# A decoder layer with 32 experts on one core: last chunk's weights split ahead, routing re-ordered, expert biases turned by TensorE

## The chip, the cores and the metric

The kernel runs on one core of one Trainium2 chip. The metric is the device time of the whole program in microseconds, lower is better. TensorE multiplies matrices, VectorE and ScalarE do elementwise work, GpSimd issues the indirect transfers, and SyncE's queue issues nearly all other transfers.

## The reference

One layer over 2048 tokens of width 1024 in fp32: three mixing branches, a gated merge, an output projection, a LayerNorm; then a router that picks 4 of 32 experts for each token, clamped-SwiGLU experts with biases, and a second LayerNorm.

```python
merged = (g_conv * (y_conv @ w_conv_proj) + g_gmlp * (y_gmlp @ w_gmlp_proj)
          + g_xa * (y_xa @ w_xa_proj))
x = layer_norm(DEEPNORM_ALPHA * x + merged @ w_out, ln1_g[l], ln1_b[l])
...
logits = (hf @ w_router + b_router).astype(jnp.float32)
top_vals, top_idx = lax.top_k(logits, TOP_K)
gate = jax.nn.softmax(top_vals, axis=-1).astype(h.dtype)
...
gu = lax.ragged_dot(xs, w_gate_up, group_sizes) + b_gate_up[sorted_expert]
g_lin, u_lin = jnp.split(gu, 2, axis=-1)
g_lin = jnp.minimum(g_lin, SWIGLU_LIMIT)
u_lin = jnp.clip(u_lin, -SWIGLU_LIMIT, SWIGLU_LIMIT)
act = (u_lin + 1) * (g_lin * jax.nn.sigmoid(SWIGLU_ALPHA * g_lin))
eo = lax.ragged_dot(act, w_down, group_sizes) + b_down[sorted_expert]
y = jnp.zeros_like(hf).at[sorted_token].add(eo * gate.reshape(-1)[order][:, None])
```

## The kernel before

Every fp32 operand is split into two parts, hi and lo: ScalarE copies the hi part (line 74), VectorE subtracts it to get the lo part (line 75), and a product is three matmuls, hi by hi, lo by hi and hi by lo. Weights come as units of 256 columns (1 MB, tile `raw`); each is split in two halves, `whi` and `wlo`. There are two `raw` buffers in the first phase and three in the experts, so a load is issued when an earlier unit has been split.

The first phase, to about 2640 us, goes over four chunks of 512 tokens. Its work is a list of items, each a weight unit with the matmuls on it (`pe`) and an epilogue (`epi`); `run_items` issues loads and splits a set number of half units ahead of the item whose matmuls it issues. A branch's last products (`proj2`, `proj3` in what follows, lines 173 to 175) are multiplied by their gates on VectorE and split (`Ah`, `Al`), because the output projection takes them as its stationary operand.

In the last chunk the output projection goes by token tiles of 128 (`last_pe`, `last_epi`): for each of four tiles 96 matmuls `lo` over two halves of the rows q and four column units j (`wo0` to `wo3`), then on VectorE the residual `r`, the LayerNorm (`ln1`) and, through TensorE, the transposes `x1T`, which are split into `Bh` and `Bl`. The router's matmuls `lg` take these. Routing of a group of tiles has three parts: `choose` makes the one-hot rows of the four chosen experts on VectorE; `place` counts each token's place with two matmuls (`pos`) and writes the lists of the experts by GpSimd; `spread` transposes the weights of the gates (`gT`). `rank` then sorts the experts by their counts, which gives `eid`, the numbers of the experts in order of size.

The experts run in a fixed order that alternates a light one (up to 128 tokens; its matmuls write `tu`, its rows are turned by `acT`) with a heavy one. Six experts are light; the heavy ones have capacities from 552 down. `schedule` puts an expert's fetch (its number, its list `lst`, its biases), the gathers of its token rows (`xg`, tiles of 128) and the preparation of each tile (`prep`: eight transposes `xsT` into two PSUM buffers, then the split into `xs`) onto the 12 steps of the expert ahead of it; with four tiles or more, the fourth preparation stands at step 10, which is step n-2. A step is one weight unit: its matmuls `up` (or `tu`), or `dn` for the down projection. All transposes, `pos`, `gT` and `lg` use one pool of two PSUM buffers, `tr_psum`.

The biases of a heavy expert's gate and up columns, `bgu`, lie with one column on each partition, since they are added per partition. `yacc` is the accumulator of the output rows in memory.

```python
self.bgu = k.sm.tile([P, 2 * KT], F32, tag="bgu", name="bgu", bufs=3)
nc.sync.dma_start(self.bgu, a["b_gate_up"][0][ds(self.reg, 1), :].rearrange("a (k p) -> p (a k)", p=P), allow_slow_non_contiguous=True)
nc.gpsimd.tensor_scalar(self.bgu[:, KT:], self.bgu[:, KT:], 1.0, None, ALU.add)
```

Of the kernel before, what the change touches and what calls it, by code (L numbers as in the profile page):

```python
# [9 lines left out]
F32 = mybir.dt.float32  # L10
F32R = mybir.dt.float32r
BF16 = mybir.dt.bfloat16
I32 = mybir.dt.int32
U32 = mybir.dt.uint32
AF = mybir.ActivationFunctionType
ALU = mybir.AluOpType
# [3 lines left out]
P = 128  # L20
D = 1024
KT = D // P
# [3 lines left out]
TT = TC // P  # L26
NE = 32
# [4 lines left out]
UC = 256  # L32
NU = D // UC
# [27 lines left out]
class Kern:  # L61
# [43 lines left out]
    def item(self, src, pe, epi=None, split=None):  # L105
        self.items.append((src, pe, epi, split or self.split_half))


    def run_items(self, first=None):
# [28 lines left out]
        for i in range(n):  # L138
            if items[i][0] is not None:
                done += 1  # L140

                split(2 * done + self.whalves - 3)
                load(ns // 2 + self.wraws)
                split(2 * done + max(2, self.whalves - 2))
            ps = items[i][1](parts.pop(i, None))

            post, self.post = self.post, []
            for f in post:
                f()
            if self.bg:  # L150
                self.bg.pop(0)()
            if items[i][2] is not None:
                items[i][2](ps)
# [47 lines left out]
    def rstd(self, pool, v, n, name, m=P):  # L201
        ve = self.nc.vector
        hv = pool.tile([P, n], F32, tag=f"hv{n}", name="hv_" + name, bufs=2)[:m]
# [330 lines left out]
    def router(self, t, th, tl):  # L534
        nc = self.nc
        te, ve = nc.tensor, nc.vector
# [5 lines left out]
        sm = self.sm  # L542
# [195 lines left out]
    def experts(self):  # L738
        exps = [Expert(self, r) for r in ORDER]

        l, h, nxt = exps[:3]
        l.number()
        h.number()

        def start(_):
            for x in (l, h):
                x.list()
            l.gather(0)
            h.gather(0)
            for x in (l, h):  # L750
                x.biases()
            l.tok_bias(0)
            l.prep(0)

# [44 lines left out]
    def overflow_table(self):  # L799
# [34 lines left out]
        ones = cp.tile([NE, P], F32, name="oones")  # L834
# [17 lines left out]
    def overflow(self):  # L852
        nc, tc = self.nc, self.tc
        n = nc.values_load(self.toti[0:1, 0:1], min_val=0, max_val=NBLK)
        with tc.For_i(0, n, 1) as i:
            e = Expert(self, None)
            e.fetch_block(i)
            e.gather(0)
            e.prep(0)
# [108 lines left out]
class Chunk:  # L968
# [12 lines left out]
    def emit(self, nxt):  # L981
# [31 lines left out]
        else:  # L1013
            self.wo = [None] * NU
            self.proj_item(2, k.vd, "pr", NU - 2)
            self.wo_item(0)
            self.wo_item(1)
            self.proj_item(2, k.vd, "pr", NU - 1)
            self.wo_item(2)
            self.wo_item(3)  # L1020
# [128 lines left out]
    def proj_item(self, b, w, src, j):  # L1149
        k = self.k  # L1150

        def pe(wt):
            return k.mm_ch(wt, *getattr(self, src), TC)
        k.item(w[:, j * UC : j * UC + UC], pe, self.proj_epi(b, j))
# [166 lines left out]
    def last_pe(self, t):  # L1321
        k, te = self.k, self.k.nc.tensor

        def pe(_):
# [3 lines left out]
            for q in range(2):  # L1328
                for j in range(NU):

                    if t >= 2 and (q, j) == (0, 1):
                        k.router(t - 2, *self.x1t[t - 2])
                    if t >= 1 and (q, j) == (1, 2):
                        self.x1_tr(t - 1)
                    hi, lo = self.wo[j][q]
# [11 lines left out]
    def last_epi(self, t):  # L1347
        k, ve = self.k, self.k.nc.vector

        def epi(ps):  # L1350
            if t == TT - 1:
                early = k.route_tasks(self.c, range(TT - 2))
                for f in early:
                    f()
            r = self.r[:, t, :]
            ve.scalar_tensor_tensor(r, r, ALPHA, ps.rearrange("p j c -> p (j c)"), ALU.mult, ALU.add)
            self.ln1(t)
            if t == TT - 1:
                third, fourth = k.route_tasks(self.c, [t - 1], ("acc", 1)), k.route_tasks(self.c, [t])
                k.router(t - 1, *self.x1t[t - 1])  # L1360
# [3 lines left out]
                k.router(t, *self.x1t[t])  # L1364
# [36 lines left out]
class Expert:  # L1401
# [22 lines left out]
    def schedule(self, n):  # L1424
# [7 lines left out]
        if self.tok:  # L1432
            todo[n - 1].append(("before", lambda: self.tok_bias(0)))
        return todo
# [17 lines left out]
    def biases(self):  # L1452
        k, nc, a = self.k, self.k.nc, self.k.a
        if self.tok:
# [3 lines left out]
            return  # L1458
        self.bgu = k.sm.tile([P, 2 * KT], F32, tag="bgu", name="bgu", bufs=3)
        nc.sync.dma_start(self.bgu, a["b_gate_up"][0][ds(self.reg, 1), :].rearrange("a (k p) -> p (a k)", p=P), allow_slow_non_contiguous=True)  # L1460
        nc.gpsimd.tensor_scalar(self.bgu[:, KT:], self.bgu[:, KT:], 1.0, None, ALU.add)
        self.xs = k.px.tile([P, KT, 2, self.C], F32R, tag="xs" + self.cls, name="xs")
# [312 lines left out]
```

## Time and profile before

| | |
|---|---|
| median of three runs | 5285.91 us (5281.21 to 5286.19) |
| profiled execution: time, span | 5280.44 us, 5278.7 us |
| mean granted TensorE clock | 0.98 of full |
| TensorE busy | 5060.7 us, 96% of the span |
| VectorE, ScalarE, GpSimd busy | 2936.3 us (56%), 2027.8 us (38%), 600.1 us (11%) |
| transfers | 794.71 MB; 766432 packets, 83416 of them under 512 bytes |

A busy share says how much of the span an engine worked; what an engine waited for, and for how long, stands in the timelines. A row of a timeline gives the start from the beginning of the span, the duration, the engine, the line of the kernel, the operation with what it writes and reads, and in brackets how long the engine was idle before it and what ended that. All times are of the one profiled execution.

### The profile page before, as it was taken

To read this page: it belongs to the slowest core of one execution; us is meant where nothing else is said; L and a number is where in the kernel's file an instruction comes from. 1 tells how busy PE (TensorE), PEld (TensorE's weight loads), DVE (VectorE), ACT (ScalarE), POOL (GpSimd) and SP (SyncE) were. 2 spreads that over 40 slices of the span, in tenths; PEclk is the share of its full clock that TensorE was granted. 3 is DMA by queue.
4 is the path that set the end of the run, shared out by engine and by line. 5 is a ranking of instruction groups with operands and counts; after the bars stand their busy time and mean duration, and the time that the engine had idled before them with its cause. 6 is when DMAs were issued, how large, how long until landed. Compare 5 with 4: busy or idle time off the path is not lost. (4 is left out here: it accounts for less than half of the span.)

```text
span 5278.7 us, 79252 instructions
## 1 busy us (share of the span) xinstructions
PE 5060.7 (96%) x32383; PEld 4633.1 (88%) x32383; DVE 2936.3 (56%) x4889; ACT 2027.8 (38%) x3011; POOL 600.1 (11%) x723
## 2 busy tenths in 40 slices
PE   9899999999999999999868999999999999999994
PEld 7788887888888888888768999999999999999984
DVE  5344346453555445543566555566666666666666
ACT  3333222332233332332234434444445555555532
POOL 0001000000010000100011112111111111211125
PEclk9899999999999999999979999999999999999997
DMA  4343332332332333322266547667666767666764
GB/s 147 123 150 132 112 112 96 112 104 93 119 109 89 112 112 104 104 88 93 87 200 205 172 127 194 187 204 205 190 181 205 207 202 207 198 205 203 210 193 128
DMA packets 766432, 794.71 MB, mean 151 GB/s; under 512 B 83416, under 2 KB 720432, under 8 KB 766064
## 3 DMA queue, kind: packets, MB, share of 16 engines
q1 hardware_dynamic: 708464, 669.78, 40.0%
q0 software_dynamic: 48000, 109.33, 8.2%
q10 hardware_dynamic: 9600, 10.49, 0.6%
q8 instruction: 257, 4.21, 0.3%
q14 instruction: 111, 0.91, 0.1%
HBM read 714.38 MB, written 75.10 MB: 150 GB/s over the span
## 5 line engine op out<-in xcount | busy, mean ns | idle before, releaser
L75 DVE TENSOR_TENSOR wlo<-raw,whi 128x1024 fp32r<-128x1024 f32 x1203 | 1450.8, 1238 | 1170.8 <-ACT whi L74 1170.5
L74 ACT ACTIVATE whi<-raw 128x1024 fp32r<-128x1024 f32 x1203 | 1220.2, 1050 | 667.0 <-PE mm L174 455.5
L173 PE MATMUL mm<-Xh,whi 128*128 128x512 f32 x1792 | 718.5, 401 | 22.1 <-ACT whi L74 22.1
L1552 PE MATMUL up<-xs,whi 128*128 128x276 f32 (+16 forms) x2304 | 724.1, 314 | 15.3 <-ACT whi L74 12.7
L1554 PE MATMUL up<-xs,wlo 128*128 128x276 f32 (+16 forms) x2304 | 721.6, 313 | 3.9 <-DVE wlo L75 3.9
L1553 PE MATMUL up<-xs,whi 128*128 128x276 f32 (+16 forms) x2304 | 720.8, 313 | 1.1 <-DVE xs L75 1.1
L175 PE MATMUL mm<-Xh,wlo 128*128 128x512 f32 x1792 | 712.9, 398 | 5.3 <-DVE wlo L75 5.2
L174 PE MATMUL mm<-Xl,whi 128*128 128x512 f32 x1792 | 708.8, 396 | 0.0
L1703 PE MATMUL dn<-whi,act 128*128 128x256 f32 (+6 forms) x2016 | 572.2, 284 | 21.1 <-ACT act L74 13.9
L1704 PE MATMUL dn<-wlo,act 128*128 128x256 f32 (+6 forms) x2016 | 569.3, 282 | 3.3 <-DVE wlo L75 3.3
L1705 PE MATMUL dn<-whi,act 128*128 128x256 f32 (+6 forms) x2016 | 568.7, 282 | 0.0
L1552 PEld LDWEIGHTS up<-xs,whi 128*128 128x128 f32 x2304 | 438.2, 190 | 24.3 <-ACT whi L74 14.4
L1734 POOL DMA_INDIRECT yacc<-yr,lst x162 | 288.9, 1783 | 1426.1 <-ACT yr L1729 1407.6
L1554 PEld LDWEIGHTS up<-xs,wlo 128*128 128x128 f32 x2304 | 438.1, 190 | 12.7 <-DVE wlo L75 6.0
L1553 PEld LDWEIGHTS up<-xs,whi 128*128 128x128 f32 x2304 | 438.5, 190 | 7.9 <-DVE xs L75 1.3
L173 PEld LDWEIGHTS mm<-Xh,whi 128*128 128x128 f32 x1792 | 338.0, 189 | 100.3 <-ACT whi L74 24.6
L175 PEld LDWEIGHTS mm<-Xh,wlo 128*128 128x128 f32 x1792 | 337.5, 188 | 91.5 <-DVE wlo L75 10.5
L174 PEld LDWEIGHTS mm<-Xl,whi 128*128 128x128 f32 x1792 | 338.2, 189 | 78.4 <-issue 0.5
L1703 PEld LDWEIGHTS dn<-whi,act 128*128 128x128 f32 (+6 forms) x2016 | 371.8, 184 | 23.4 <-ACT act L74 14.4
L1704 PEld LDWEIGHTS dn<-wlo,act 128*128 128x128 f32 (+6 forms) x2016 | 371.8, 184 | 4.8 <-DVE wlo L75 4.5
L1705 PEld LDWEIGHTS dn<-whi,act 128*128 128x128 f32 (+6 forms) x2016 | 371.7, 184 | 0.4 <-DVE act L75 0.4
L1548 PE MATMUL up<-xs,whi 128*128 128x352 f32 (+7 forms) x1280 | 370.0, 361 | 0.0
(402 smaller groups left out, 9023.4 us busy)
## 6 DMA issues: line engine op xcount, KB each, us to landing
raw<-in_w_gate_up SPq DMA_DIRECT2D x256, 1024.0 KB, 5.5
raw<-in_w_in SPq DMA_DIRECT2D x131, 1024.0 KB, 5.0
raw<-in_w_down SPq DMA_DIRECT2D x128, 1024.0 KB, 6.3
raw<-in_w_conv_proj SPq DMA_DIRECT2D x16, 1024.0 KB, 5.2
raw<-md SPq DMA_DIRECT2D x16, 1024.0 KB, 5.2
raw<-in_w_gmlp_proj SPq DMA_DIRECT2D x16, 1024.0 KB, 5.1
raw<-vd SPq DMA_DIRECT2D x16, 1024.0 KB, 5.3
raw<-in_w_out SPq DMA_DIRECT2D x16, 1024.0 KB, 6.2
```

What stands on the lines that cost most here:

```text
L74: self.nc.scalar.activation(hi, src, AF.Copy)
L75: self.nc.vector.tensor_tensor(lo, src, hi.bitcast(F32), ALU.subtract)
L173: te.matmul(o, hi[:, k, cs], xh[:, kk, :], start=first, stop=False)
L174: te.matmul(o, hi[:, k, cs], xl[:, kk, :], start=False, stop=False)
L175: te.matmul(o, lo[:, k, cs], xh[:, kk, :], start=False, stop=last)
L1548: te.matmul(o, hi[:, kk, cs], xv, start=first, stop=False)
L1552: te.matmul(o, hi[:, kk, cs], xs[:, kg, 0, s0:s1], start=first, stop=False)
L1553: te.matmul(o, hi[:, kk, cs], xs[:, kg, 1, s0:s1], start=False, stop=False)
L1554: te.matmul(o, lo[:, kk, cs], xs[:, kg, 0, s0:s1], start=False, stop=last)
L1703: te.matmul(o, ah, hi[:, kk, :], start=first, stop=False)
L1704: te.matmul(o, ah, lo[:, kk, :], start=False, stop=False)
L1705: te.matmul(o, al, hi[:, kk, :], start=False, stop=last)
```

## The change

It has five parts.

A. In the last chunk the item order becomes proj2, proj3, wo0 to wo3 instead of proj2, wo0, wo1, proj3, wo2, wo3, and proj3's item lets three more half units be split ahead of its matmuls (`ahead=3`; the method `item` stores the number).

B. The transposes of a tile's rows stand at the column unit (1, 1) of the next tile instead of (1, 2). The router's matmuls of a tile are issued ahead of the next tile's epilogue, its VectorE part in `router_tile`. For tiles 0 and 1, `choose` is issued in the epilogue of tile 2, `place` at (0, 2) of tile 3's matmuls and `spread` at (1, 3), where before all three stood ahead of tile 3's residual. The reciprocal root of one column takes 9 VectorE operations instead of 13.

C. The numbers and lists of the first two experts are issued ahead of the first expert weights.

D. `bgu` is no longer loaded by columns: the row of 2048 values is loaded as 16 rows of 128 (`brow`), TensorE turns it (`bT`, into a buffer of `tr_psum`), and VectorE copies one half and adds 1 to the other. This `bias_turn` stands after step n-2; the block of overflow experts and the first heavy expert call it on their own.

E. In the overflow table a tile of ones is taken from an existing buffer (not shown).

```diff
@@ -141,7 +142,7 @@
                 split(2 * done + self.whalves - 3)
                 load(ns // 2 + self.wraws)
-                split(2 * done + max(2, self.whalves - 2))
+                split(2 * done + max(2, self.whalves - 2) + items[i][4])
             ps = items[i][1](parts.pop(i, None))
             post, self.post = self.post, []
...
@@ -200,6 +201,19 @@
     def rstd(self, pool, v, n, name, m=P):
         ve = self.nc.vector
+
+        if n == 1:
+            h = pool.tile([P, n], F32, tag=f"hv{n}", name="hv_" + name, bufs=2)[:m]
+            ve.tensor_scalar(h, v, -0.5, -0.5 * EPS, ALU.mult, ALU.add)
+            y = pool.tile([P, n], F32, tag=f"y{n}", name="y_" + name, bufs=2)[:m]
+            s = pool.tile([P, n], F32, tag=f"s{n}", name="s_" + name, bufs=2)[:m]
+
+            ve.tensor_scalar(s.bitcast(I32), h.bitcast(I32), 1, None, ALU.logical_shift_right)
+            ve.tensor_scalar(y.bitcast(I32), s.bitcast(I32), -1.0, float(0x5F3759DF - 0x400000 + 0x40000000), ALU.mult, ALU.add)
+            for _ in range(3):
+                ve.scalar_tensor_tensor(s, y, h, y, ALU.mult, ALU.mult)
+                ve.scalar_tensor_tensor(y, s, 1.5, y, ALU.add, ALU.mult)
+            return y
         hv = pool.tile([P, n], F32, tag=f"hv{n}", name="hv_" + name, bufs=2)[:m]
         ve.tensor_scalar(hv, v, EPS, None, ALU.add)
         y = pool.tile([P, n], F32, tag=f"y{n}", name="y_" + name, bufs=2)[:m]
...
@@ -532,14 +546,16 @@
     def router(self, t, th, tl):
-        nc = self.nc
-        te, ve = nc.tensor, nc.vector
+        te = self.nc.tensor
         ps = self.tr_psum("lg")
         for k in range(KT):
             wv = self.wr[:, k, :, :].rearrange("p h e -> p (h e)")
             te.matmul(ps[:, : 2 * NE], th[:, k, :], wv, start=k == 0, stop=False)
             te.matmul(ps[:, : 2 * NE], tl[:, k, :], wv, start=False, stop=k == KT - 1)
-        sm = self.sm
+        return ps
+
+    def router_tile(self, t, ps):
+        ve, sm = self.nc.vector, self.sm
         if t == 0:
             self.v8 = sm.tile([P, TT, 8], F32, tag="v8", name="v8")
             self.i8 = sm.tile([P, TT, 8], U32, tag="i8", name="i8")
...
@@ -739,18 +755,20 @@
         exps = [Expert(self, r) for r in ORDER]
         l, h, nxt = exps[:3]
+
         l.number()
+        l.list()
         h.number()
+        h.list()
         def start(_):
-            for x in (l, h):
-                x.list()
             l.gather(0)
             h.gather(0)
             for x in (l, h):
                 x.biases()
             l.tok_bias(0)
             l.prep(0)
+            h.bias_turn()
         def prep(t):
             h.prep(t)
...
@@ -1013,11 +1033,10 @@
         else:
             self.wo = [None] * NU
             self.proj_item(2, k.vd, "pr", NU - 2)
-            self.wo_item(0)
-            self.wo_item(1)
-            self.proj_item(2, k.vd, "pr", NU - 1)
-            self.wo_item(2)
-            self.wo_item(3)
+
+            self.proj_item(2, k.vd, "pr", NU - 1, 3)
+            for j in range(NU):
+                self.wo_item(j)
             for t in range(TT):
                 k.item(None, self.last_pe(t), self.last_epi(t))
...
@@ -1328,10 +1347,12 @@
             for q in range(2):
                 for j in range(NU):
-                    if t >= 2 and (q, j) == (0, 1):
-                        k.router(t - 2, *self.x1t[t - 2])
-                    if t >= 1 and (q, j) == (1, 2):
+                    if t >= 1 and (q, j) == (1, 1):
                         self.x1_tr(t - 1)
+                    if t == TT - 1 and (q, j) == (0, 2):
+                        self.early[1]()
+                    if t == TT - 1 and (q, j) == (1, 3):
+                        self.early[2]()
                     hi, lo = self.wo[j][q]
                     for kk in range(4):
                         kg = q * 4 + kk
...
@@ -1348,20 +1369,22 @@
         k, ve = self.k, self.k.nc.vector
         def epi(ps):
-            if t == TT - 1:
-                early = k.route_tasks(self.c, range(TT - 2))
-                for f in early:
-                    f()
+            lg = k.router(t - 1, *self.x1t[t - 1]) if t else None
+            if 0 < t < TT - 1:
+                k.router_tile(t - 1, lg)
             r = self.r[:, t, :]
             ve.scalar_tensor_tensor(r, r, ALPHA, ps.rearrange("p j c -> p (j c)"), ALU.mult, ALU.add)
             self.ln1(t)
+            if t == TT - 2:
+                self.early = k.route_tasks(self.c, range(TT - 2))
+                self.early[0]()
             if t == TT - 1:
                 third, fourth = k.route_tasks(self.c, [t - 1], ("acc", 1)), k.route_tasks(self.c, [t])
-                k.router(t - 1, *self.x1t[t - 1])
+                k.router_tile(t - 1, lg)
                 third[0]()
                 self.x1_tr(t)
                 third[1]()
-                k.router(t, *self.x1t[t])
+                k.router_tile(t, k.router(t, *self.x1t[t]))
                 fourth[0]()
                 fourth[1]()
                 k.rank()
...
@@ -1431,6 +1454,7 @@
             todo[p].append(("after", lambda t=t: self.prep(t)))
         if self.tok:
             todo[n - 1].append(("before", lambda: self.tok_bias(0)))
+        todo[n - 2].append(("after", self.bias_turn))
         return todo
...
@@ -1456,10 +1480,20 @@
             if self.m < P // 2:
                 nc.vector.memset(self.xs[:, :, :, self.m :].bitcast(F32), 0.0)
             return
+        self.brow = k.sm.tile([2 * KT, P], F32, tag="brow", name="brow")
+        nc.sync.dma_start(self.brow, a["b_gate_up"][0][ds(self.reg, 1), :].rearrange("a (k p) -> (a k) p", p=P))
+        self.xs = k.px.tile([P, KT, 2, self.C], F32R, tag="xs" + self.cls, name="xs")
+
+
+    def bias_turn(self):
+        k, nc = self.k, self.k.nc
+        if self.tok:
+            return
+        pt = k.tr_psum("bT")[:, : 2 * KT]
+        nc.tensor.transpose(pt, self.brow, k.ident[: 2 * KT, : 2 * KT])
         self.bgu = k.sm.tile([P, 2 * KT], F32, tag="bgu", name="bgu", bufs=3)
-        nc.sync.dma_start(self.bgu, a["b_gate_up"][0][ds(self.reg, 1), :].rearrange("a (k p) -> p (a k)", p=P), allow_slow_non_contiguous=True)
-        nc.gpsimd.tensor_scalar(self.bgu[:, KT:], self.bgu[:, KT:], 1.0, None, ALU.add)
-        self.xs = k.px.tile([P, KT, 2, self.C], F32R, tag="xs" + self.cls, name="xs")
+        nc.vector.tensor_copy(self.bgu[:, :KT], pt[:, :KT])
+        nc.vector.tensor_scalar(self.bgu[:, KT:], pt[:, KT:], 1.0, None, ALU.add)
     def both(self, name):
...
```

The order of instructions on the engines shows where this comes to stand. First ScalarE at the end of the last chunk, from the gates of proj2's branch on, before: `Xh` and `whi` of the units wo0 and following, `Ah` the merged products' hi part.

```order
L1171 ACTIVATE gate<-mm,chan 128x512 x2
L74 ACTIVATE whi<-raw 128x1024 x2
L1171 ACTIVATE gate<-mm,chan 128x512 x2
L74 ACTIVATE Xh<-raw 128x1024 x2
L74 ACTIVATE Ah<-M 128x512 x2
L74 ACTIVATE Xh<-raw 128x1024 x2
L74 ACTIVATE whi<-raw 128x1024 x4
L74 ACTIVATE Ah<-M 128x512 x2
L74 ACTIVATE whi<-raw 128x1024
L74 ACTIVATE Bh<-raw 128x4x256
```

And now:

```order
L1190 ACTIVATE gate<-mm,chan 128x512 x2
L74 ACTIVATE whi<-raw 128x1024 x2
L1190 ACTIVATE gate<-mm,chan 128x512 x2
L74 ACTIVATE whi<-raw 128x1024 x2
L74 ACTIVATE Ah<-M 128x512 x2
L74 ACTIVATE Xh<-raw 128x1024 x4
L74 ACTIVATE whi<-raw 128x1024
L74 ACTIVATE Ah<-M 128x512 x2
L74 ACTIVATE whi<-raw 128x1024 x2
L74 ACTIVATE Bh<-raw 128x4x256
```

A pair of `whi`, proj3's weights, moved ahead of the first `Ah`, the two pairs of `Xh` (wo0 and wo1) behind it are together, and a `whi` of the next unit stands ahead of the second `Ah`, proj3's.

Second, TensorE at the routing of tiles 0 and 1, which stood behind the last matmul of tile 3 before:

```order
L1341 MATMUL lo<-Bh,Ah 128x256
L1342 MATMUL lo<-Bl,Ah 128x256
L1343 MATMUL lo<-Bh,Al 128x256
L627 LDWEIGHTS lower
L627 MATMUL pos<-rscr,lower 128x64
L628 LDWEIGHTS ones_b
L628 MATMUL pos<-rscr,ones_b 128x64
L673 MATMUL gT<-ident,rscr_19579 96x128 x2
L540 MATMUL lg<-wr,Bh 128x64
L541 MATMUL lg<-wr,Bl 128x64
L540 MATMUL lg<-wr,Bh 128x64
```

It now stands among tile 3's matmuls, 24 behind their begin:

```order
L1362 MATMUL lo<-Xh,Ah 128x256
L1363 MATMUL lo<-Xl,Ah 128x256
L1364 MATMUL lo<-Xh,Al 128x256
L643 LDWEIGHTS lower
L643 MATMUL pos<-rscr,lower 128x64
L644 LDWEIGHTS ones_b
L644 MATMUL pos<-rscr,ones_b 128x64
L1362 MATMUL lo<-whi,Ah 128x256
L1363 MATMUL lo<-wlo,Ah 128x256
L1364 MATMUL lo<-whi,Al 128x256
```

`pos` moved ahead of 72 of the tile's matmuls; `gT` follows later, at (1, 3).

Third, TensorE at the end of the preparation of the expert with 460 tokens, before: the light expert's `tu`, the last tile's transposes, then the down matmuls.

```order
L1578 MATMUL tu<-whi,xs 96x256
L1579 MATMUL tu<-wlo,xs 96x256
L1580 MATMUL tu<-whi,xs 96x256
L1527 MATMUL xsT<-ident,xg 128x76 x8
L1703 MATMUL dn<-whi,act 128x256
L1704 MATMUL dn<-wlo,act 128x256
L1705 MATMUL dn<-whi,act 128x256
```

And now:

```order
L1612 MATMUL tu<-whi,xs 96x256
L1613 MATMUL tu<-wlo,xs 96x256
L1614 MATMUL tu<-whi,xs 96x256
L1561 MATMUL xsT<-ident,xg 128x76 x8
L1493 MATMUL bT<-ident,brow 128x16
L1737 MATMUL dn<-whi,act 128x256
L1738 MATMUL dn<-wlo,act 128x256
```

`bT` came between the transposes and the down matmuls; the same stands at the other four experts with four tiles or more. On VectorE the two reads of it follow the split of that tile:

```order
L75 TENSOR_TENSOR wlo<-raw,whi 128x1024 x2
L1624 TENSOR_TENSOR Xt<-tu,bb 96x256
L1631 TENSOR_SCALAR Xt<-Xt 96x256
L75 TENSOR_TENSOR wlo<-raw,whi 128x1024 x2
L75 TENSOR_TENSOR xs<-xsT,xs 128x4x76 x2
L1495 COPY bgu<-bT 128x8
L1496 TENSOR_SCALAR bgu<-bT 128x8
L1624 TENSOR_TENSOR ut<-tu,bb 96x256
```

Only the rows of `bgu` are new there; what stands ahead of `xs` is as before.

## Rows read from the trace of the kernel before

**Rows 1.** Busy time by windows, inside the experts; the first line names the columns.

```profile
core 0: us, PE busy (x) PEld busy (x) DVE busy (x) ACT busy (x) POOL busy (x), PEclk, DMA share, GB/s
...
3600.00:3700.00 100.00, 100.00 (x740) 99.72 (x739) 65.20 (x106) 51.82 (x88) 14.11 (x14) 1.00 0.66 197
```

**Rows 2.** Timeline of TensorE, last chunk: start, duration, instruction, idle time before and releaser.

```profile
2559.60 0.80 PE L173 MATMUL mm<-Bh,whi 128*128 128x512 f32 x1 [7.73 <-ACT whi L74]
...
2574.13 0.28 PE L1341 MATMUL lo<-Xh,Ah 128*128 128x256 f32 x1
2574.25 0.28 PE L1342 MATMUL lo<-Xl,Ah 128*128 128x256 f32 x1
...
2580.13 0.38 PE L1341 MATMUL lo<-whi,Ah 128*128 128x256 f32 x1 [1.55 <-ACT whi L74]
...
2581.39 0.38 PE L1342 MATMUL lo<-wlo,Ah 128*128 128x256 f32 x1 [0.88 <-DVE wlo L75]
...
2634.59 0.63 PE L673 MATMUL gT<-ident,rscr 128*96 128x128 f32 x2 [4.52 <-DVE rscr L667]
```

**Rows 3.** Busy time by windows behind two waits of TensorE; PEclk is the granted clock.

```profile
2559.00:2566.00 7.00, 5.99 (x14) 4.26 (x15) 3.31 (x3) 1.97 (x3) 0.00 (x0) 0.51 0.72 238
...
2634.00:2636.00 2.00, 1.41 (x8) 1.43 (x8) 1.88 (x4) 0.43 (x2) 1.65 (x4) 0.52 0.01 1
```

**Rows 4.** Timeline of VectorE, last chunk and routing.

```profile
2588.82 1.22 DVE L1356 SCALAR_TENSOR_TENSOR r<-r,lo 128x1024 f32<-128x1024 f32 x1 [6.35 <-DMA r<-in_x]
...
2615.03 1.22 DVE L1356 SCALAR_TENSOR_TENSOR r<-r,lo 128x1024 f32<-128x1024 f32 x1 [1.35 <-PE lo L1343]
...
2627.66 0.15 DVE L602 TENSOR_TENSOR gt<-v 128x8 f32<-128x8 f32 x1
...
2630.11 0.49 DVE L632 TENSOR_TENSOR rscr<-pos,rscr 128x128 f32<-128x128 f32 x2
...
2634.33 1.21 DVE L1356 SCALAR_TENSOR_TENSOR r<-r,lo 128x1024 f32<-128x1024 f32 x1
...
2642.71 0.14 DVE L602 TENSOR_TENSOR gt<-v 128x4 f32<-128x4 f32 x1
```

**Rows 5.** Timelines of SyncE's queue, GpSimd and TensorE, start of the experts.

```profile
2661.24 0.90 SPq L1450 DMA_DIRECT2D lst<-lists  x2
...
2669.49 0.96 POOL L1516 DMA_INDIRECT xg<-x1d,lst  x1 [9.52 <-DMA yacc<-r]
...
2676.23 1.07 PE L1527 MATMUL xsT<-ident,xg 52*128 52x52 f32 x8 [10.66 <-DMA bb<-in_b_gate_up]
```

**Rows 6.** DMA issues by line: count, KB of each, median us to landing.

```profile
lst<-lists SPq DMA_DIRECT2D x32, 16.0 KB, 1.6
...
bgu<-in_b_gate_up SPq DMA_DIRECT2D x26, 8.0 KB, 2.9
```

**Rows 7.** Waits of TensorE in the experts: us in total, times, longest.

```profile
PE xsT L1527 <- DMA xg<-x1d,lst: 4.2, 2, 2.9
```

**Rows 8.** Timelines of TensorE and VectorE, last prep of four of the five large experts.

```profile
2845.40 0.36 PE L1703 MATMUL dn<-whi,act 128*128 128x256 f32 x1
...
2852.10 1.28 DVE L75 TENSOR_TENSOR xs<-xsT,xs 128x512 fp32r<-128x512 f32 x2
...
3036.85 0.36 PE L1703 MATMUL dn<-whi,act 128*128 128x256 f32 x1
...
3041.18 1.28 DVE L75 TENSOR_TENSOR xs<-xsT,xs 128x512 fp32r<-128x512 f32 x2
...
3400.92 0.39 PE L1703 MATMUL dn<-whi,act 128*128 128x256 f32 x1
...
3404.55 0.48 DVE L75 TENSOR_TENSOR xs<-xsT,xs 128x128 fp32r<-128x128 f32 x2
...
5030.69 0.36 PE L1703 MATMUL dn<-whi,act 128*128 128x256 f32 x1
...
5032.02 0.98 DVE L75 TENSOR_TENSOR xs<-xsT,xs 128x368 fp32r<-128x368 f32 x2
```

**Rows 9.** Timeline of TensorE behind the first of these.

```profile
2857.59 0.65 PE L1527 MATMUL xsT<-ident,xg 40*128 40x40 f32 x4 [1.84 <-DVE act L75]
```

More of the change, by code (lines that the diff above doesn't have):

```diff
@@ L103, in split_half, with item @@
         return hi, lo
-    def item(self, src, pe, epi=None, split=None):
-        self.items.append((src, pe, epi, split or self.split_half))
+    def item(self, src, pe, epi=None, split=None, ahead=0):
+        self.items.append((src, pe, epi, split or self.split_half, ahead))
     def run_items(self, first=None):
@@ L833, in overflow_table @@
         ve.tensor_scalar(mk[:, 2, :], mk[:, 0, :], self.iota_c, None, ALU.mult)
-        ones = cp.tile([NE, P], F32, name="oones")
+        ones = room[:, : NE + NBLK]
         ve.memset(ones, 1.0)
@@ L858, in overflow @@
             e.gather(0)
+            e.bias_turn()
             e.prep(0)
@@ L1147, in gate_item, with proj_item @@
         self.k.item(self.wcol(COL_G + b * D, j), self.zx, self.gate_epi(b, j))
-    def proj_item(self, b, w, src, j):
+    def proj_item(self, b, w, src, j, ahead=0):
         k = self.k
@@ L1153, in pe @@
             return k.mm_ch(wt, *getattr(self, src), TC)
-        k.item(w[:, j * UC : j * UC + UC], pe, self.proj_epi(b, j))
+        k.item(w[:, j * UC : j * UC + UC], pe, self.proj_epi(b, j), ahead=ahead)
     def projections(self, b, w, src, js):
```

## The prediction

> **What bounds the kernel now.** The page comes first: TensorE is busy for 96% of the span. The busy time by windows then says where it isn't: inside the experts it is busy for 100.00 of 100 us [rows 1], so there a microsecond that it is made to wait is a microsecond of the span, unless a later wait takes it up. Slack lies at the turn from the last chunk to the experts (about 2550 to 2800 us) and in the last norms. So I read the timelines of that turn, and then the places in the experts where the change puts an instruction into TensorE's row. The sum is made against the profiled execution, 5280.4 us (span 5278.7 and 1.7 around it); the median of the runs, 5285.9, lies 5.5 above it. A difference of 0.2%, 10.6 us, is about what a measurement of this kernel can tell from none.
>
> **A, the output weights split ahead.** Before, TensorE stands 7.73 us for proj3's first weights, and 1.55 and 0.88 us for the last output weights [rows 2]. After the first of these the granted clock is 0.51 over 7 us [rows 3], the 1.2 GHz level: 7 x 0.49 = 3.4 us lost, some 0.5 of it while idle, so about 2.9. That makes 10.2 us of waits and 2.9 of clock to be removed. I do not give all of it back. The first wait goes: proj3's whi is now ahead of the two gate epilogues in ScalarE's row. But the raw buffer for wo2 is released only by wo0's split, ScalarE now has a whi of a wo unit ahead of proj3's `Ah`, and so proj3's epilogue on VectorE starts late and wo3's split comes behind it. Laying the old durations into the new order, I find new waits of 0.9 + 1.2 us for wo2 and 5.2 + 1.3 us for wo3. The first tile's `r`, at 2588.82 before [rows 4], comes at 2583.3 to 2585.5. **A: -3.3 to -5.5; I take -4.3.**
>
> **B, the routing chain.** What it removes: before, VectorE does choose and place of tiles 0 and 1 (from 2627.66) ahead of tile 3's `r` (2634.33) [rows 4], and TensorE waits 4.52 us for their `gT` [rows 2]. Tile 2's `r` stands at 2615.03, so 19.3 us lie between the two. What it adds: `pos` now stands in TensorE's own row behind the first 24 output matmuls of tile 3, and it needs choose, which is queued on VectorE behind tile 2's whole LayerNorm. One such matmul is 0.12 us (2574.13 to 2574.25 [rows 2]). From tile 2's end TensorE has 16 router matmuls, smaller, so at most 1.9, and 24 x 0.12 = 2.9: 4.8 us. VectorE waits for the router (1.9), then does its router tile and LayerNorm (2634.33 to 2642.71 is 8.4 for the same two; four small operations fewer in the reciprocal root, which I put at 0.5) and choose (2627.66 to 2630.11, 2.45): 12.2 us. So TensorE stands about 7.4 us, and 72 matmuls, the next transposes and `gT` are queued behind the `pos` that waits. Tile 3's `r` comes 12.2 + 72 x 0.12 + about 1.6 for ten transposes (four small ones take 0.65 [rows 9]) = 22.4 us after tile 2's end, 3.1 later than before; 2.9 more where the clock falls; and the transposes of tiles 0 and 1, one step forward, meet a LayerNorm that still runs, up to 2 us. **B: +3.1 to +8.0; I take +6.3**, since 4.52 us of waiting at this very place did bring the clock to 0.52 [rows 3].
>
> **C, lists first.** The two list loads were issued at 2661.24, behind a 1 MB weight unit; the gather starts at 2669.49, and xsT stands 10.66 us until the gathered rows are there [rows 5]. A list load takes 1.6 us in the median [rows 6], so issued first the lists are there near 2663. The gather then waits for what is next late, the last rows of the accumulator, near 2666: -3.3 us. The weight unit behind the lists starts 0.7 later, which xsT's wait covers; were it not covered, C would be -2.6. **C: -3.3, or 0 where something else holds the gather.**
>
> **D, the biases as rows, is what costs.** The 26 `bgu` loads land 2.9 us after issue [rows 6]; GpSimd waits for each, with gathers queued behind it. But TensorE's waits for gathered rows are 4.2 us in all of the experts [rows 7], and that is the ceiling of what a freer GpSimd and emptier queues can give: -3, with 0 and -4.2 as ends.
>
> In their place come 26 transposes, and what matters is where they stand. In five experts, those of four tiles or more (capacities 552, 532, 460, 416 and 476), `bT` stands in TensorE's row right behind the last prep (eight xsT, two PSUM buffers) and ahead of the down matmuls. It takes one of the same two buffers, so the prep's first one must be free, and it is free when VectorE has made the first half of `xs`. VectorE reaches that late, behind two pairs of `wlo`. Before, TensorE did not care: it went straight on to `dn`, which needs nothing of this prep. Both ends are in the trace [rows 8]: when `dn` started, and when `xs` did, half of whose row frees the buffer.
> - 552: 2852.10 + 0.64 - 2845.40 = 7.3
> - 532: 3041.18 + 0.64 - 3036.85 = 5.0, and the 460 reads like it, 5.0
> - 416: 3404.55 + 0.24 - 3400.92 = 3.9
> - 476: 5032.02 + 0.49 - 5030.69 = 1.8
>
> Together 23.0 us. ScalarE and VectorE go on meanwhile, so the next waits shrink (1.84 us at 2857.59 behind the first stall [rows 9]): **+21, with 18 and 23 as ends.** The other 21 find a free buffer. Their nearest row is four transposes of 40 columns in 0.65 us [rows 9], 0.16 each, or 3.5 for the 21 with the bubble that a change of weights leaves (2.5 to 5). The two small reads on VectorE lie beside full TensorE work.
>
> **The clock behind the stalls.** After the wait of 4.52 us, which followed full work, the granted clock was 0.52, after the one of 7.73 us 0.51 over 7 us [rows 2, 3]. Four of the five stalls are of 3.9 us or more; at 2.9 each that is **+11** (0 to 11.6).
>
> Sum: -4.3 + 6.3 - 3.3 - 3.0 + 21 + 3.5 + 11 = +31.2, and 5280.4 + 31.2 = 5311.6: **5312 us**.
>
> **A rule that speaks for the change.** A `bgu` of 8 KB, 4-byte pieces, lands in 2.9 us, a list of 16 KB in 1.6 [rows 6]. The Trainium skill, page "DMA: Bandwidth & Descriptors", section "Specifications", says that a transfer comes to line rate only with 512 bytes and more in a piece; by that rule the old load was the costly one, and rows of 512 bytes mend it. The trace agrees in that the small pieces take longer. By the rows the load is hidden, and the sum has 3 us for it; what it would be otherwise is the fourth rival.
>
> **The rivals.**
> - The buffer is free in time, on the other side: VectorE reaches `xs` before TensorE reaches `bT` at the five places, and the 21 and the 11 fall away: 5279.6, no change. It decides where VectorE's lag, 3.9 to 7.3 us, is used up by earlier weights. Against it: the two `wlo` pairs stand ahead of `xs` in the new order too, and between ScalarE's splits stand activations that wait for VectorE, not for a load. Chance 0.16; a third of it with the turn gaining too, near 5268.
> - The stalls come, but the clock holds: 5300.6. For it: a fall is shown for 4.52 and 7.73 us, not for 3.9, and not among down matmuls. Chance 0.15.
> - The turn gains all that the old rows offer: no wait at `pos` or wo3, and the 13.1 us of A and 5.4 of B come back; against the -4.3 and +6.3 of the sum that is 20 less: 5291. Against it: choose stands behind 8 us of VectorE's row. Chance 0.09.
> - The small loads held up more than GpSimd: 26 x (2.9 - 1.6) = 34 us of landing, all on the path: 5281. Against it: TensorE is busy for 100 of 100 us while such loads go on [rows 1]. By the Trainium skill's rule above this would be the likely case. Chance 0.05.
> - Worse: new waits at the turn are followed by half clock once more, and the stalls take nothing back from later waits: +9, 5321. Chance 0.10.
>
> The forecast keeps 0.45. Faster by over 0.2% takes 0.06 (of the first rival), within 0.2% 0.24 (the rest of the first, the third and the fourth), slower 0.70. With about 1 in 10 left out at each end the range is 5280 to 5328; the forecast's own, from its bounds, is 5300 to 5324.
>
> **What would show it.** Right: waits of TensorE ahead of `bT` of about 7, 5, 5, 4 and 2 us that end with VectorE's `xs`, half clock behind the first four; a wait of some 7 us at `pos`; proj3 without its 7.73; the first gather some 3 us nearer to the expert numbers. Wrong: `bT` without idle time (first rival), `pos` without a wait (third), or TensorE's waits unchanged and the end earlier (fourth).

## The result and the profile after

The changed kernel takes 5315.42 us (median of four runs, 5312.26 to 5317.33), the kernel before 5286.05 in the runs taken with it: a ratio of 1.0056, 95% interval 1.0039 to 1.0073. The profiled execution took 5312.26 us, its span is 5310.5, 31.8 us more than before.

The page has TensorE at the same 96% of a longer span, and 53 thousand small packets fewer:

```profile
PE 5079.1 (96%) x32409; PEld 4647.4 (88%) x32409; DVE 2928.8 (55%) x4805; ACT 2028.4 (38%) x3011; POOL 585.9 (11%) x697
...
DMA packets 713598, 794.70 MB, mean 150 GB/s; under 512 B 30168, under 2 KB 667600, under 8 KB 713232
```

The small packets went, and the time grew; so the first view to open is TensorE's timeline at the places where the change put something into its row. These are the turns `bT` of the five large experts, each with the first `dn` behind it, which answers to the `dn` rows of [rows 8]:

```profile
2853.76 0.28 PE L1493 MATMUL bT<-ident,brow 16*128 16x16 f32 x1 [4.94 <-DVE xs L75]
2853.97 0.58 PE L1737 MATMUL dn<-whi,act 128*128 128x256 f32 x1
...
3046.18 0.28 PE L1493 MATMUL bT<-ident,brow 16*128 16x16 f32 x1 [4.82 <-DVE xs L75]
3046.39 0.58 PE L1737 MATMUL dn<-whi,act 128*128 128x256 f32 x1
...
3246.54 0.28 PE L1493 MATMUL bT<-ident,brow 16*128 16x16 f32 x1 [4.89 <-DVE xs L75]
...
3422.08 0.28 PE L1493 MATMUL bT<-ident,brow 16*128 16x16 f32 x1 [3.91 <-DVE xs L75]
3422.30 0.58 PE L1737 MATMUL dn<-whi,act 128*128 128x256 f32 x1
...
5063.40 0.23 PE L1493 MATMUL bT<-ident,brow 16*128 16x16 f32 x1 [1.71 <-DVE xs L75]
5063.56 0.39 PE L1737 MATMUL dn<-whi,act 128*128 128x256 f32 x1
```

In brackets stand five waits of 20.3 us together, each ended by VectorE's `xs`. The duration of the `dn` behind them tells of the clock: 0.58 us at the lower level behind the first four, 0.39 behind the last. The windows behind the stalls say the same, with the granted clock third from the end:

```profile
2853.50:2860.00 6.50, 6.24 (x40) 6.21 (x41) 4.76 (x10) 1.01 (x2) 0.00 (x0) 0.74 0.59 176
...
3046.00:3052.00 6.00, 5.82 (x28) 5.79 (x29) 4.17 (x9) 0.93 (x1) 0.00 (x0) 0.53 0.63 192
...
3246.00:3252.50 6.50, 5.96 (x38) 5.93 (x39) 4.40 (x10) 1.16 (x2) 0.00 (x0) 0.74 0.63 185
...
3422.00:3428.00 6.00, 5.92 (x31) 5.88 (x32) 3.79 (x9) 0.60 (x1) 0.00 (x0) 0.57 0.67 199
...
5063.00:5069.00 6.00, 5.60 (x47) 5.58 (x47) 4.39 (x13) 2.84 (x5) 0.00 (x0) 1.00 0.54 178
```

The time lost in the first four is the length of a window times one less the clock: 1.7 + 2.8 + 1.7 + 2.6 = 8.8 us.

A running ledger needs only rows that both traces have. The distance of after from before is -1.2 us at the first xsT of the experts (2675.03 against 2676.23 [rows 5]), +8.6 at the `dn` behind the first stall (2853.97 against 2845.40 [rows 8]), +9.5 and +21.4 behind the second and the fourth (3046.39, 3422.30), +32.9 behind the last (5063.56), and +31.8 at the end. So all of the loss lies inside the experts. The -1.2 holds -1.6 that stood already at the last matmul of the gate item ahead of proj2 (2538.70 against 2540.27). The biases alone (below), whose first phase is that of the kernel before, stand at 2544.64 there; so a few us of difference at that place come without any edit. Of the 11.5 us between the fourth stall and the last, some 7 come without any wait. The same transpose stands at 3567.25 in the trace before and at 3591.43 after, +24.2, and another at 4992.48 and 5023.26, +30.8; first the trace before, then the trace after:

```profile
3567.25 0.35 PE L1613 MATMUL acT<-ident,ut 112*128 112x112 f32 x2
...
4992.48 1.03 PE L1527 MATMUL xsT<-ident,xg 128*128 128x128 f32 x8
```

```profile
3591.43 0.35 PE L1647 MATMUL acT<-ident,ut 112*128 112x112 f32 x2
...
5023.26 1.04 PE L1561 MATMUL xsT<-ident,xg 128*128 128x128 f32 x8
```

Nineteen turns lie between the two, and the distance grows by 6.6 us, 0.35 for each.

The place where the distance shrinks most lies behind the first stall. In the trace before, TensorE waits there by itself (1.84 us at 2857.59 [rows 9], and the row below), and its clock falls:

```profile
2855.21 0.30 PE L1613 MATMUL acT<-ident,ut 64*128 64x64 f32 x2 [1.43 <-DVE ut L1607]
...
2857.00:2861.00 4.00, 3.41 (x16) 3.34 (x17) 1.92 (x6) 1.80 (x5) 1.74 (x2) 0.50 0.61 190
```

After the change the same two transposes wait 0 and 0.47 us, and the window from 2860 to 2864 has full clock:

```profile
2863.16 0.34 PE L1647 MATMUL acT<-ident,ut 64*128 64x64 f32 x2
...
2864.19 0.44 PE L1561 MATMUL xsT<-ident,xg 40*128 40x40 f32 x4 [0.47 <-DVE act L75]
...
2860.00:2864.00 4.00, 3.72 (x33) 3.47 (x32) 0.16 (x1) 0.47 (x2) 0.00 (x0) 1.00 0.72 238
```

So the distance falls from +9.4 ahead of the first of them (2862.95 against 2853.50) to +4.3 behind the second (2867.34 against 2863.00): 5.1 us of the first stall and its clock are given back, 2.8 as shorter waits and 2.3 as clock that only the kernel before loses there.

At the turn from the last chunk to the experts, the timeline of TensorE after shows the waits that took the place of [rows 2]:

```profile
2564.89 0.38 PE L1362 MATMUL lo<-whi,Ah 128*128 128x256 f32 x1 [0.52 <-ACT whi L74]
2566.15 0.39 PE L1363 MATMUL lo<-wlo,Ah 128*128 128x256 f32 x1 [0.88 <-DVE wlo L75]
2572.74 0.58 PE L1362 MATMUL lo<-whi,Ah 128*128 128x256 f32 x1 [5.04 <-ACT whi L74]
2574.19 0.58 PE L1363 MATMUL lo<-wlo,Ah 128*128 128x256 f32 x1 [0.86 <-DVE wlo L75]
2605.41 1.06 PE L1420 MATMUL x1T<-ident,r 128*128 128x128 f32 x8 [1.04 <-DVE r L241]
2622.12 0.24 PE L643 MATMUL pos<-rscr,lower 128*128 128x64 bf16 x1 [6.73 <-DVE rscr L634]
```

The 7.73 us ahead of proj3 are gone, 7.3 us stand ahead of wo2 and wo3 instead, and 6.73 at `pos`, where the clock is granted at 0.50:

```profile
2622.00:2626.00 4.00, 3.60 (x17) 3.49 (x18) 3.45 (x20) 0.00 (x0) 0.00 (x0) 0.50 0.16 66
```

On VectorE the `r` of tiles 0, 2 and 3, on GpSimd the first gather and on TensorE the first xsT answer to [rows 4, 5]:

```profile
2582.82 1.22 DVE L1376 SCALAR_TENSOR_TENSOR r<-r,lo 128x1024 f32<-128x1024 f32 x1 [7.54 <-PE lo L1364]
...
2613.34 1.20 DVE L1376 SCALAR_TENSOR_TENSOR r<-r,lo 128x1024 f32<-128x1024 f32 x1
...
2635.15 1.22 DVE L1376 SCALAR_TENSOR_TENSOR r<-r,lo 128x1024 f32<-128x1024 f32 x1 [2.96 <-PE lo L1364]
...
2667.00 0.94 POOL L1550 DMA_INDIRECT xg<-x1d,lst  x1 [6.54 <-PE gb L700]
...
2675.03 1.06 PE L1561 MATMUL xsT<-ident,xg 52*128 52x52 f32 x8 [8.92 <-DMA xg<-x1d,lst]
```

Tile 0's `r` is 6.0 us earlier, tile 3's 0.8 later; the gather is 2.5 earlier and what it brings only 1.2.

### The profile page after: what moved, and what is told of

It reads as the page before. It is cut to its first block, busy times and chain, and to the rows that moved or that the text cites. A ratio compares the mean times of both kernels' runs of the same rounds, so it can differ in the third digit from the quotient of the medians.

```text
span 5310.5 us, 79174 instructions
## 1 busy us (share of the span) xinstructions
PE 5079.1 (96%) x32409; PEld 4647.4 (88%) x32409; DVE 2928.8 (55%) x4805; ACT 2028.4 (38%) x3011; POOL 585.9 (11%) x697
```

## The experiments

Eight kernels follow. The first four ran on one chip, beside 27 runs of the kernel before with a median of 5286.13 us. The last four ran on another chip, on which the kernel before itself took 5315.49 (21 runs); their times are read as ratios to that.

**The turn one step later.** In the five large experts the turn stands behind the down matmuls of the next unit, so that TensorE has work while VectorE makes `xs`.

```diff
-        todo[n - 2].append(("after", self.bias_turn))
+        if self.T >= 4:
+            todo[n - 1].insert(0, ("after", self.bias_turn))
+        else:
+            todo[n - 2].append(("after", self.bias_turn))
```

> The changed kernel, but in the five experts with four tiles or more the turn of the biases stands one step later, behind the down matmuls and ahead of a fifth tile's preparation; the other 21 turns stay. Theory (the cost is the wait for the prep's PSUM buffer and the half clock behind it): the five waits ahead of bT, 4.94 + 4.82 + 4.89 + 3.91 + 1.71 = 20.3 us, go to under 2 us together, the granted clock behind them stays at 1.00 (some 9 us in four places), and some 4 us that later waits gave back are lost again: 5315 - 25 = 5290 us, 5286 to 5294. Rival 1 (the cost is the transposes and their reads on VectorE, wherever they stand): 5310 or more. Rival 2 (the turn from the last chunk to the experts costs it): 5310 or more.

Measured: 5289.1 us (11 runs), ratio 1.0007, interval 0.9998 to 1.0016, inside the range of the theory. TensorE's waits by line, from 2790 to 5070 us, hold one at a turn:

```profile
PE bT L1496 <- DVE xs L75: 0.4, 1, 0.4
```

and the window behind the first large expert's last preparation has full clock, where it fell before the edit:

```profile
2853.00:2860.00 7.00, 7.00 (x62) 7.00 (x60) 5.36 (x9) 5.18 (x7) 0.00 (x0) 1.00 0.53 165
```

So have the windows behind the next three (3041 to 3047, 3233 to 3240 and 3400 to 3406 us). Five instructions moved by one step give back 26 of the 29 us between the medians. Nearly all of the cost was where the turn stood, not that it was made; both rivals expected 5310 or more and are out.

**The biases alone.** The kernel before with only part D (and part E, for room).

```diff
-        self.bgu = k.sm.tile([P, 2 * KT], F32, tag="bgu", name="bgu", bufs=3)
-        nc.sync.dma_start(self.bgu, a["b_gate_up"][0][ds(self.reg, 1), :].rearrange("a (k p) -> p (a k)", p=P), allow_slow_non_contiguous=True)
-        nc.gpsimd.tensor_scalar(self.bgu[:, KT:], self.bgu[:, KT:], 1.0, None, ALU.add)
+        self.brow = k.sm.tile([2 * KT, P], F32, tag="brow", name="brow")
+        nc.sync.dma_start(self.brow, a["b_gate_up"][0][ds(self.reg, 1), :].rearrange("a (k p) -> (a k) p", p=P))
...
+        todo[n - 2].append(("after", self.bias_turn))
```

> The kernel before with only the biases as rows turned by TensorE (and the tile of ones out of an existing buffer, for room); the last chunk, the routing and the order of the lists as before. Theory: all of the loss is in this part, and the other parts together give -1 us at the start of the experts: 5286 + 33 = 5319 us, 5314 to 5323, with five waits ahead of bT of 5 to 7.3 us and 1.7. Rival (the last chunk's re-ordering costs a third or more of the loss): below 5308.

Measured: 5316.54 us (5 runs), ratio 1.0059, interval 1.0046 to 1.0073. The first and the last of the stalls in the experts' timeline of TensorE:

```profile
2858.35 0.28 PE L1472 MATMUL bT<-ident,brow 16*128 16x16 f32 x1 [5.98 <-DVE xs L75]
...
5069.09 0.23 PE L1472 MATMUL bT<-ident,brow 16*128 16x16 f32 x1 [1.71 <-DVE xs L75]
```

Part D alone costs what the whole change costs. The time is inside the theory's range, and the rival (under 5308) is out.

**Everything but the biases.** The changed kernel with the biases by columns: the edit shown for the biases alone, read from + to -, in the changed kernel.

> The changed kernel with the biases loaded by columns as before; last chunk, routing and lists as changed. Theory: first xsT of the experts 1 to 2 us earlier than in the kernel before, the rest as before: 5285 us, 5281 to 5288. Rival (the re-ordered last chunk costs a third or more of the loss): 5296 or more.

Measured: 5284.87 us (11 runs), ratio 1.0000, interval 0.9991 to 1.0009, as the theory had it; the rival (5296 or more) is out. The other parts together come to nothing that the times can tell. The two experiments add up: +30.4 and -1.3 us against their chip's median, 29.1, where the whole change gave 29.4.

**The transpose three times.** On the kernel with the late turn.

```diff
-        nc.tensor.transpose(pt, self.brow, k.ident[: 2 * KT, : 2 * KT])
+        for _ in range(3):
+            nc.tensor.transpose(pt, self.brow, k.ident[: 2 * KT, : 2 * KT])
```

> The kernel with the late turn, in which each of the 26 transposes of biases is done three times into the same buffer, so two more each. Theory (each turn costs TensorE 0.3 us or more wherever it stands, as the growing distance of 0.35 us an expert in the changed kernel's trace shows, and half of it is the transpose itself): 52 more at 0.13 to 0.23 us, 7 to 12 us slower than the kernel with the late turn. Rival (the distance grows through something else, VectorE's reads or the row loads): under 4 us slower.

Measured: 5293.98 us (11 runs), 4.9 us over the kernel with the late turn: 0.09 for each of 52 more, below what the theory expected and above the rival. The intervals of the two ratios (0.9998 to 1.0016 and 1.0005 to 1.0023) overlap, so the times alone don't decide; the rows do. First a place of the kernel before where the change puts a turn, then that turn of the changed kernel, then a turn of this kernel:

```profile
3706.56 0.24 PE L1549 MATMUL up<-xs,wlo 128*128 128x160 f32 x1
3706.63 0.32 PE L1703 MATMUL dn<-whi,act 128*128 128x256 f32 x1
3706.79 0.28 PE L1704 MATMUL dn<-wlo,act 128*128 128x256 f32 x1
```

```profile
3731.08 0.24 PE L1583 MATMUL up<-xs,wlo 128*128 128x160 f32 x1
3731.25 0.23 PE L1493 MATMUL bT<-ident,brow 16*128 16x16 f32 x1
3731.41 0.39 PE L1737 MATMUL dn<-whi,act 128*128 128x256 f32 x1
3731.63 0.28 PE L1738 MATMUL dn<-wlo,act 128*128 128x256 f32 x1
```

```profile
3799.06 0.32 PE L1592 MATMUL up<-xs,wlo 128*128 128x344 f32 x1
3799.31 0.35 PE L1497 MATMUL bT<-ident,brow 16*128 16x16 f32 x3
3799.59 0.39 PE L1741 MATMUL dn<-whi,act 128*128 128x256 f32 x1
```

From the start of `bT` to the next matmul it is 0.16 us with one transpose and 0.28 with three, 0.06 for each more; 52 more of these make 3.1 us. The theory had half of the price in the transpose itself; by the rows it is 0.06 of 0.35, and the rest is the break in the stream. From the last `up` to the second `dn` the kernel before takes 0.23 us and the changed kernel 0.55, which is 0.32 more: 0.17 from `up` to `bT`, 0.16 to the first `dn` and 0.22 to the second, in place of 0.07 and 0.16.

**The weights alone.** The kernel before with part A.

```diff
-            self.wo_item(0)
-            self.wo_item(1)
-            self.proj_item(2, k.vd, "pr", NU - 1)
-            self.wo_item(2)
-            self.wo_item(3)
+            self.proj_item(2, k.vd, "pr", NU - 1, 3)
+            for j in range(NU):
+                self.wo_item(j)
```

> The kernel before with only the output weights split ahead. Theory: counted from proj2's first matmul, the first output matmul comes 11 us earlier (22.6 instead of 33.4 to 33.9 us) and tile 0's r 4 us earlier, since waits of 0.5, 0.9, 5.0 and 0.9 us stand in tile 0's matmuls; tile 0's r to the expert numbers stays at 69.6 us. Rival (the waits for wo2 and wo3 come from the routing part, not from this one): r 10 us earlier.

**The routing alone.** The kernel before with part B, less the shorter root.

```diff
+                    if t == TT - 1 and (q, j) == (0, 2):
+                        self.early[1]()
+                    if t == TT - 1 and (q, j) == (1, 3):
+                        self.early[2]()
...
+            lg = k.router(t - 1, *self.x1t[t - 1]) if t else None
+            if 0 < t < TT - 1:
+                k.router_tile(t - 1, lg)
```

> The kernel before with only the routing chain re-ordered (the reciprocal root as before). Theory: from tile 0's r to the expert numbers 75.5 us instead of 69.6, with a wait of 6.5 to 7.5 us ahead of pos and half clock behind it; up to tile 0's r as before. Rival (the wait at pos comes from the weights split ahead): 66 us or less.

Each has one run alone (5311.53 and 5329.27 us on the second chip), so they are read from their timelines. The stretches, worked out as differences of starts, in us; "proj2" is the start of the last matmul of the gate item ahead of it, "eid" the start of TensorE's matmul that gives the expert numbers:

| kernel | proj2 to tile 0's r | r of tile 0 to r of tile 3 | r of tile 0 to eid | eid to first gather | eid to first xsT |
|---|---|---|---|---|---|
| before | 48.55 | 45.51 | 69.62 | 11.05 | 17.79 |
| changed | 44.12 | 52.33 | 76.15 | 8.03 | 16.06 |
| biases alone | 49.47 | 45.62 | 69.63 | 11.00 | 18.46 |
| all but the biases | 44.56 | 51.00 | 74.58 | 8.03 | 15.27 |
| late turn | 44.95 | 51.25 | 75.08 | 8.03 | 15.21 |
| weights alone | 44.94 | 45.64 | 69.76 | 10.59 | 16.65 |
| routing alone | 49.21 | 56.17 | 80.17 | 10.74 | 17.89 |
| late turn, late place | 44.43 | 43.74 | 67.71 | 8.03 | 15.53 |
| late place, no turn | 45.01 | 43.74 | 67.49 | 8.03 | 15.02 |

The weights alone do what was expected of them: -3.6 us to tile 0's `r`, with the waits of 5.04 and 0.59 us for wo3 and wo2 in their own timeline, and nothing behind that. The routing alone costs more than expected, 80.2 us instead of 75.5. Its wait at `pos` is 7.14 us, in the range; but tile 3's `r` comes 15.6 us behind `pos` where the changed kernel has 13.0, and its row puts 5.72 us of waiting on a releaser that the profile doesn't name:

```profile
2663.54 0.24 PE L629 MATMUL pos<-rscr,lower 128*128 128x64 bf16 x1 [7.14 <-DVE rscr L620]
...
2678.98 0.29 PE L540 MATMUL lg<-wr,Bl 128*128 128x64 f32 x1 [0.52 <-issue]
```

```profile
2679.17 1.22 DVE L1359 SCALAR_TENSOR_TENSOR r<-r,lo 128x1024 f32<-128x1024 f32 x1 [5.72 <-remote]
```

TensorE's last `lo` starts at 2676.09 there, 12.6 us behind `pos`, where the changed kernel has 12.7 (2634.83); so the 2.6 us more come behind tile 3's last `lo`. It is one run, and what held VectorE there stays open.

**Late turn and late place.** `pos` at the last column unit of tile 3, `gT` behind tile 3's LayerNorm, the transposes where they were.

```diff
-                    if t >= 1 and (q, j) == (1, 1):
+                    if t >= 1 and (q, j) == (1, 2):
                         self.x1_tr(t - 1)
-                    if t == TT - 1 and (q, j) == (0, 2):
-                        self.early[1]()
                     if t == TT - 1 and (q, j) == (1, 3):
-                        self.early[2]()
+                        self.early[1]()
...
                 k.router_tile(t - 1, lg)
+                self.early[2]()
```

> The kernel with the late turn of the biases, and pos of tiles 0 and 1 five column units later in tile 3's matmuls, at (1, 3) instead of (0, 2); gT behind tile 3's LayerNorm instead of at (1, 3), the transposes of a tile's rows at (1, 2) as before. Theory (pos waits for choose, which is ready 12 us after tile 2's end, whatever TensorE has done by then): the wait of 6.73 us at pos goes to under 1 us, the clock behind it stays at 1.00, tile 3's r comes some 44 us after tile 0's r instead of 51 to 52 (before: 45.5), and the time goes down by 6 to 8 us, to 5282. Rival (the wait only moves: VectorE's place now stands ahead of tile 3's r and delays it by as much as the wait): tile 3's r 49 us or more after tile 0's, 5287 or more.

Measured: ratio 0.9997, interval 0.9988 to 1.0006 (11 runs, 5313.97 against 5315.49 us). Tile 3's `r` comes 43.74 us after tile 0's, `pos` has no wait, and the experts' first xsT is 7.6 us earlier than with the late turn alone, counted from proj2. By the rows the theory is right and the rival (49 us or more) out. The times don't decide it: 0.9997 against 1.0007 is 5 us, measured on two chips, with intervals that overlap. And three things moved at once, `pos`, `gT` and the transposes, so what each is worth isn't shown.

**Late place, no turn.** The same with the biases by columns.

> The same late pos and gT, with the biases loaded by columns as in the kernel before: weights split ahead, routing chain, lists first, nothing turned by TensorE. Theory: 6 to 8 us less than the version without the turned biases (5285), so 5278, and 0.1 to 0.2% faster than the kernel before. Rival (what is gained at the turn is lost again at the first weights, which wait for their transfers): 5284 or more.

Measured: ratio 0.9989, interval 0.9980 to 0.9998 (11 runs, 5309.78 against 5315.49 us), the lowest ratio of all and inside the theory's 0.1 to 0.2%. The rival, 5284 or more, would be 0.9996 or more, and the interval doesn't quite shut it out; nor does it part this kernel from the one without the turns and with the early place (1.0000, 0.9991 to 1.0009). The timeline of TensorE has `pos` without a wait, and 1.49 us left at `gT`:

```profile
2655.44 0.19 PE L643 MATMUL pos<-rscr,lower 128*128 128x64 bf16 x1
...
2660.38 0.39 PE L689 MATMUL gT<-ident,rscr 128*96 128x128 f32 x2 [1.49 <-DVE rscr L683]
```

The difference between these two, 0.0008 of 5315 us, is 4 us where the 26 turns at 0.35 would make 9. The other such pair, the late turn and everything but the biases, differs by 4.2 us as well. The rows have a part of the answer: the kernel with turns waits 0.69 us for gathered rows at 3393.20 where the one without waits 3.17, so the turned biases also give something back, 2.5 us at that place.

## Why the prediction held, term by term

The forecast was 5312 us by a sum of +31.2 on the profiled execution; the trace gave +31.8, and the medians +29.4. The mechanism that carries the sum, the stalls at the turns with half clock behind them, was the one named. That the sum came within 0.6 us is partly luck: several terms were off by about 2 to 4 us, and the errors offset each other.

- **Stalls at the turns: +21, measured 20.3 in the rows and 17.5 net.** The 21 was 23.0 of stalls less 2 for shorter waits behind them. Four of the five stalls are within 0.2 us of the working. The first was worked out at 7.3 and came at 4.94, for a reason that the sum did not have: TensorE arrived 3.2 us late (xsT at 2847.78 instead of 2844.61), VectorE's `xs` only 0.9 late (2853.02 against 2852.10 [rows 8]). So this stall shrank by what TensorE had lost just before. With the biases alone it was 5.98. The shorter waits behind the first stall gave back 2.8.
- **Clock: +11, measured 8.8** in the windows behind the stalls. The fall came behind all four stalls of 3.9 us or more and not behind the one of 1.7. The rival in which the clock holds is out. The sum had neither the fall at 2840 us ahead of the first stall (2.7 us, last section) nor the 2.3 that only the kernel before loses behind it; with both it is 9.2.
- **The 26 transposes: +3.5, too small by half.** Each costs 0.35 us and not 0.16, 7.3 for the 21 outside the large experts' last preparation (two of which also wait, 0.47 us at 2676.56 and 0.42 at 3580.69). The step that was mis-sized was to price one by a quarter of a row of four: the row of four hides the break at its two ends, and that break is most of the price, as the rows of the tripled transposes show.
- **Relief for GpSimd and the queues: -3, measured -2.5** in TensorE's waits for gathered rows inside the experts, which went from 4.2 us to 1.7 [rows 7]. But a loss that the sum had no term for eats it up: from the first xsT (-1.2) to 2755 us (+1.2) the distance grows by 2.4, with new waits of 0.96 and 0.87 us for the first weights (2686.41 and 2687.67). Everything but the biases waits at those matmuls too (1.12 and 0.87 us), so these waits are not the turns'.
- **A: -4.3, measured -4.4** in the changed kernel (44.12 against 48.55) and -3.5 to -4.1 in the others. Of 10.2 us of waits removed, 7.3 came back at wo2 and wo3, where the order had been worked out to give 8.6. Half clock came back too, behind the wait of 5.04 (the `lo` rows of 0.58 us), and for that the working had no term.
- **B: +6.3, measured +6.5** (76.15 against 69.62), 5.0 and 5.5 in the two others of the table with this place of `pos` and with A, and 10.6 in the routing alone. The wait at `pos` was put at 7.4 and is 6.73. But the 6.5 lies elsewhere than in the working, which had 6.0 of it between the `r` of tiles 2 and 3 and at most 2 ahead of that. There it is 21.81 us instead of 19.30, +2.5 with the half clock; between tiles 0 and 2 it is 30.52 instead of 26.21, +4.3; and behind tile 3 -0.3. So the agreement in the total is luck. With the late place the same routing is 2 us faster than before instead of 6.5 slower, so choosing early was not what cost; which of the three moved pieces did isn't shown.
- **C: -3.3, measured -1.7.** The gather does start 3.0 us earlier after the expert numbers (8.03 against 11.05) in every kernel with the lists first. But from the gather to xsT it took 8.03 us instead of 6.74, and the sum had taken that stretch as fixed.

Put together: -1.6 that stood before, +0.4 of A, B and C, +2.4 at the first weights, -2.5, 17.5, 9.2 and 7.3, and -1.1 behind the last stall make 31.6, against the 31.8 of the trace.

Of the rivals, the free buffer is out in the changed kernel and is what the late turn makes of it. Its 5279.6 was counted from the profiled execution, 5.7 us below the median of the runs; from the median it would be 5285.3, and the late turn's 5289.1 lies 3.8 above that, which the turns' higher price can account for. The rival in which the turn gains all is out by the waits of 6.73 us at `pos` and 5.04 at wo3, and the one in which the small loads were on the path by the time itself. Of the worse rival, the half clock behind the new waits came (0.50 at `pos`), its +9 did not. The rule on small pieces that the prediction cites (the Trainium skill, page "DMA: Bandwidth & Descriptors", section "Specifications": line rate from 512 bytes) said that the old loads were the costly ones. 53 thousand packets under 512 bytes are gone, and by the trace it did not matter here, since the loads lay beside a full TensorE, and the kernel with the lowest ratio, the late place without the turns, still has them.

## What to carry to other kernels

Before an instruction is put into the row of the engine that bounds a kernel, read from the trace when the buffer or operand that it needs is ready, not only how long it takes: here a transpose of 0.16 us cost 5, because everything behind it in TensorE's row had nothing to do with what it waited for. Such a piece belongs as far behind its producer as its consumer allows; one step was enough for the turns, five column units for `pos`. And a transfer that nobody on the bounding engine waits for is not made cheaper by moving it onto that engine.

## What the runs showed that I had not expected

- A lone small transpose in a stream of matmuls costs 0.35 us, and two more beside it 0.06 each: the break costs more than the work.
- The largest stall cost the least on balance: the first took 4.94 us and the clock, and behind it 5.1 us were given back within 5 us, since the kernel before lost them there on its own.
- The clock fell where nothing in the waits differs. Ahead of the xsT at 2840 us both kernels wait 1.43 and 1.49 us; before, the window 2840 to 2845 has full clock, after it has half, and 2.7 us go there (the distance grows from +0.5 to +3.2). What decides it isn't shown. First the trace before, then the trace after:

```profile
2840.00:2845.00 5.00, 4.70 (x40) 4.71 (x41) 2.62 (x7) 3.08 (x6) 1.08 (x2) 1.00 1.05 347
```

```profile
2840.00:2845.00 5.00, 4.24 (x20) 4.24 (x21) 2.83 (x6) 2.15 (x5) 1.07 (x2) 0.50 1.05 338
```

- One chip and another gave 5286 and 5315 us for the kernel before, 0.55% apart, as much as the change itself; only comparisons on one chip tell the change.
